# A one-layer gated mixer on one core: mask and one-hot products grouped, one output tile summed in another order, one tile group given more banks

## The chip, the core and the metric

The kernel runs on one core of one Trainium2 chip. A core has TensorE (PE, matrix products into eight PSUM banks), VectorE (DVE), ScalarE (ACT), GpSimd (POOL) and SyncE (SP, which here only issues DMAs). Each engine works through its own instructions in order and waits on semaphores for the others. The metric is the device time of one execution in microseconds (us); the figure to compare is the median of several runs.

## The reference

One decoder layer over 512 tokens of width 1024, all in float32:

```python
def mixer(x, ...):
    proj = x @ w_in                       # q, k, v of three branches and three gate vectors
    o_da  = diff_attention(...)           # 4 heads, two softmax maps each, relative bias
    o_sb  = stick_breaking_attention(...) # 8 heads of 64, strictly causal
    o_dl  = dilated_attention(...)        # 12 heads of 128, windows with stride 1, 4, 16, relative bias
    merged = g0 * (o_da @ w_branch_da) + g1 * (o_sb @ w_branch_sb) + g2 * (o_dl @ w_branch_dil)
    return merged @ w_out

x   = layer_norm(ALPHA * x + mixer(x))
c   = square(relu(x @ w_up)) @ w_down
ple = sigmoid(x @ w_ple_gate) * (p @ w_ple)
x   = layer_norm(ALPHA * x + c + ple)
```

In stick-breaking attention a query sees only earlier keys: `before = k_pos < q_pos` masks the logits. The relative bias is `bias_table[rel_bucket(distance)]`, with 32 buckets and 16 heads that use a bias.

## The kernel before

Nearly every product is split: an operand is held as a high and a low part (each of a type that PE takes at full rate), and three products hi·hi, hi·lo, lo·hi are added in PSUM. A weight chunk of 128×1024 comes by a DMA of SP into a ring tile `raw`, ACT rounds it to `wh` (L243), DVE subtracts to get `wl` (L245), and PE multiplies. Several large products are formed by seven products of sums instead of eight; the sums of weights are added up in DRAM by DMAs of POOL.

The work is one list of `items`. The loop over it emits, for each item, some weight splits (`pump`, whose second argument is how many at most), one step of each attention head in flight (`step`), and the item's products; the result of an item is read out while the next one runs. What stands in an engine's queue in the end is this emission, put in order again by the tile framework, which also chooses the PSUM banks: six banks are for `at_bank()` tiles and two for `mm_bank()` tiles.

The places that the change touches:

- `sb_head` (L1601 on): one head of the stick-breaking branch, eight in all, between 20 and 230 us. It takes three banks for the logits: `bank[2]` holds two key blocks (`kb` 3 and 2) side by side, `bank[1]` and `bank[0]` one each. Per key block it makes a pair of products (`mm_pair`, lines L146 and L147) and then adds the mask by a product of the bf16 identity `identb` with `mask_b` (256 columns for key block 3, 128 for the others; lines L1613 and L1616). ACT (L1628) reads the bank next.
- `rel_vec` and `tables` (L1480, L1519): the bias as a function of distance. The bias table `rel`, split into three bf16 parts on 96 partitions and a row of −1e30 on the 97th, is multiplied with one-hot columns `oh`: five products of four heads each, every one with a bank, an ACT copy (L1485) and a POOL DMA to the DRAM tile `rv` of its own. `shifted` later reads `rv` back.
- `wout_items` (L877): the output projection, per half of the columns four token tiles `tt` of eight contraction steps `k`. Step `k` reads `merged_T[k // 4, tt // 2, ...]`, which `turn_item` makes by four transposes on PE (L794), a cast on ACT (`mh`, L798) and a subtraction on DVE (`ml`, L799). The order of items is tile 0, turns (1,1,·), tile 1, turns (0,1,·), tile 2, tile 3.
- `ple_items` (L945): the embedding product `p @ w_ple`, eight tiles `(half, tt)`, each in an `at_bank()`, read out by ACT (L961). Between them PE transposes the normed tokens (L924), also into `at_bank()` tiles.

Of the kernel before, what the change touches and what calls it, by code (L numbers as in the profile page):

```python
# [12 lines left out]
BF16 = mybir.dt.bfloat16  # L13
# [3 lines left out]
S = 512  # L17
D = 1024
P = 128
# [36 lines left out]
def trunk(tc, a, out):  # L56
    nc = tc.nc
    es = ExitStack()
    with es:
# [14 lines left out]
        def slot(name, dt=F32):  # L74
            return big.tile([P, 512], dt, name=nm(name), tag="s", bufs=NSLOT)
# [7 lines left out]
        def at_bank():  # L83
            return psum.tile([P, 512], F32, name=nm("at"), tag="at", bufs=6)
# [58 lines left out]
        def mm_pair(ps, st, tw, side, cs, cm, start, stop):  # L143

            hi, lo = tw[side]
            nc.tensor.matmul(ps, st[side][:, cs], hi[:, cm], start=start, stop=False, skip_group_check=True)  # L146
            nc.tensor.matmul(ps, st[side][:, cs], lo[:, cm], start=False, stop=stop, skip_group_check=True)  # L147
# [107 lines left out]
        def pump(limit, most=2):  # L255
            n = 0
            while n < most and st["split"] < len(chunks) and st["split"] < limit + RING:
                fill()
                issue_split()
                n += 1  # L260
            fill()
# [4 lines left out]
        def item(cs, mm, ev, need=None, bank=None, size=1.0):  # L266
            items.append({"c": cs, "mm": mm, "ev": ev, "need": need, "bank": bank, "size": size})
# [17 lines left out]
        T = {}  # L285
# [517 lines left out]
        last_plain = len(items)  # L803
# [73 lines left out]
        def wout_items():  # L877
            for half in range(2):
                cs = [chunk(a["wo"][half, c].rearrange("p k n -> p (k n)"), 1024) for c in range(4)]
                for tt in range(4):  # L880
                    def mm(ps, tt=tt, cs=cs):
                        for k in range(8):
                            c = cs[k // 2]
                            s = slice((k % 2) * 512, (k % 2) * 512 + 512)
                            h, lo = merged_T[k // 4, tt // 2, k % 4 // 2]
                            q = slice(k % 2 * 256 + tt % 2 * P, k % 2 * 256 + tt % 2 * P + P)
                            nc.tensor.matmul(ps, h[:, q], c["h"][:, s], start=k == 0, stop=False)
                            nc.tensor.matmul(ps, h[:, q], c["l"][:, s], start=False, stop=False)
                            nc.tensor.matmul(ps, lo[:, q], c["h"][:, s], start=False, stop=k == 7)

                    def ev(ps, tt=tt, half=half):
                        y = xn.pop((tt, half))
                        if not half:
                            x1sum[tt] = small("lsm", 2)
                        i = nc.vector.scalar_tensor_tensor(y, y, ALPHA, ps, op0=OP.mult, op1=OP.add,
                                                           accum_out=x1sum[tt][:, half:half + 1])
                        st["added"] = getattr(i, "ins", i)
                        x1[tt, half] = y
                        if half:
                            pending.append(ln1_gen(tt))  # L900
                    item(cs if tt == 3 else [], mm, ev, need=cs, bank=at_bank)
                    for t in {0: [(1, 1, 0), (1, 1, 1)], 1: [(0, 1, 0), (0, 1, 1)]}.get(tt, ()) if not half else ():
                        turn_item(*t)
# [41 lines left out]
        def ple_items():  # L945
            cs = [chunk(a["wp"][half].rearrange("p k n -> p (k n)"), 1024) for half in range(2)]
            for half in range(2):
                for tt in range(4):
                    def mm(ps, tt=tt, half=half):
                        c = cs[half]  # L950
                        for k in range(2):
                            s = slice(k * 512, k * 512 + 512)
                            q = slice(tt * P, tt * P + P)
                            h, lo = pTs[k]
                            nc.tensor.matmul(ps, h[:, q], c["h"][:, s], start=k == 0, stop=False)
                            nc.tensor.matmul(ps, h[:, q], c["l"][:, s], start=False, stop=False)
                            nc.tensor.matmul(ps, lo[:, q], c["h"][:, s], start=False, stop=k == 1)

                    def ev(ps, tt=tt, half=half):
                        t = slot("ple")  # L960
                        nc.scalar.copy(t, ps)  # L961
                        ple[tt, half] = t
                    item([cs[half]] if tt == 3 else [], mm, ev, need=cs, bank=at_bank)


        sums_first = set()
# [463 lines left out]
        ple_at = len(items)  # L1430
# [17 lines left out]
        identb = one.tile([P, P], BF16, name="identb")  # L1448
# [13 lines left out]
        mask_b = one.tile([P, 2, P], BF16, name="mask_b")  # L1462
# [13 lines left out]
        rel = one.tile([97, 16], BF16, name="rel")  # L1476
        nc.vector.memset(rel[96:97, :], NEG)
        rv = dram.tile([16, 640], F32, name="rv")

        def rel_vec(cols, segs):  # L1480
            for src, d0, n in segs:
                ps = at_bank()
                nc.tensor.matmul(ps[0:4, :n], rel[:, cols], src, start=True, stop=True)
                sb = slot("rvs")[0:4, :]
                nc.scalar.copy(sb[:, :n], ps[0:4, :n])  # L1485
                nc.gpsimd.dma_start(rv[cols, d0:d0 + n], sb[:, :n])
                yield

        def shifted(h0, n, m):
            ts = []  # L1490
# [19 lines left out]
        tab_da = tab_g0 = tab_g1 = tab_g2 = None  # L1510

        oh = []

        def load_onehot():
            oh.extend(slot("oh", BF16) for _ in range(3))
# [2 lines left out]

        def tables():  # L1519
            nonlocal tab_g0, tab_g1, tab_g2  # L1520
            yield from rel_vec(slice(0, 4), [(oh[0][:97, :], 0, 512), (oh[1][:97, 0:128], 512, 128)])
            yield from rel_vec(slice(4, 8), [(oh[1][:97, 128:512], 0, 384)])
            yield from rel_vec(slice(8, 12), [(oh[2][:97, 0:256], 0, 256)])
            yield from rel_vec(slice(12, 16), [(oh[2][:97, 256:512], 0, 256)])
            tab_g0 = shifted(4, 4, 256)
            tab_g1 = shifted(8, 4, 128)
            tab_g2 = shifted(12, 4, 128)
# [34 lines left out]
        def make_lam():  # L1562
            lamt, t, r = lams

            nc.vector.tensor_copy(rel[0:32, :], t)
            nc.vector.tensor_sub(t, t, rel[0:32, :])
            nc.vector.tensor_copy(rel[32:64, :], t)
            nc.vector.tensor_copy(r, rel[32:64, :])
            nc.vector.tensor_sub(t, t, r)
            nc.vector.tensor_copy(rel[64:96, :], t)  # L1570
            lp = one.tile([P, 2], F32, name="lp")
            for i in range(2):
                nc.vector.scalar_tensor_tensor(lamt[:, 2 * i, :], lamt[:, 2 * i, :], 1.0, lamt[:, 2 * i + 1, :],
                                               op0=OP.mult, op1=OP.mult, accum_out=lp[:, i:i + 1])
            nc.scalar.activation(lp, lp, AF.Exp)
            nc.vector.tensor_sub(lam, lp[:, 0:1], lp[:, 1:2])
            nc.vector.tensor_scalar(lam, lam, LAM_INIT, -1.0, op0=OP.add, op1=OP.mult)
            nc.vector.tensor_scalar(gcol, gcol, 1.0 - LAM_INIT, None, op0=OP.mult)
# [22 lines left out]
        def sb_head(hd):  # L1601
            pr, side = hd // 2, hd % 2
# [3 lines left out]
            blk = [(0, 0, 0, 512), (1, 1, 0, 384), (2, 2, 0, 256), (3, 2, 256, 256)]  # L1606
            bank = [at_bank() for _ in range(3)]
            for kb, bi, c0, n in reversed(blk):
                ps = bank[bi][:, c0:c0 + n]
                mm_pair(ps, T["sb_k", pr], T["sb_q", pr], side, slice(kb * P, kb * P + P), slice(S - n, S),  # L1610
                        kb != 2, False)
                if kb == 3:
                    nc.tensor.matmul(ps, identb, mask_b.rearrange("p a b -> p (a b)"), start=False, stop=False,  # L1613
                                     skip_group_check=True)
                else:
                    nc.tensor.matmul(ps[:, 0:P], identb, mask_b[:, 1, :], start=False, stop=False,  # L1616
                                     skip_group_check=True)
            w = [512, 384, 512]
            sph, spl, later = {}, {}, {}
            for bi in (2, 1, 0):  # L1620
                n = w[bi]
                ps = bank[bi][:, :n]
# [9 lines left out]
                h = slot("sph", F32R)[:, :n]  # L1632
                lo = slot("spl", F32R)[:, :n]
# [24 lines left out]
            for kb, bi, c0, n in reversed(blk):  # L1658
                ps = bank[bi][:, c0:c0 + n]
# [305 lines left out]
        for n, it in enumerate(items):  # L1965
# [22 lines left out]
                for _ in range(lead):  # L1988
                    left_step(*preps.popleft())

            pump(freed, {1: 3, 3: 0, 4: 0, ple_at: 0, ple_at + 1: 0}.get(n, 1 if n < 10 else 2))
            if n == 8:
                tie.clear()
            if n == 4:
# [158 lines left out]
```

## Time and profile before

| | |
|---|---|
| median of three runs | 1042.58 us (1042.33 to 1043.28) |
| time of the profiled execution | 1043.19 us |
| its span, first to last instruction | 1041.0 us |
| mean granted clock of TensorE | 0.998 |
| PE busy | 1031.1 us, 99% |
| DVE busy | 787.0 us, 76% |
| ACT busy | 593.2 us, 57% |
| POOL busy | 180.0 us, 17% |

A row of the timeline gives the start, the duration, the engine, the line and operation, the tiles written and read, their shape (for a product first the weights, partitions*columns, then what streams through, partitions x columns) and, in brackets, the idle time ahead with the engine that ended it. Products are pipelined: what one of them costs is read from the start of one row to the start of the next, since the durations overlap. PEld rows are the loads of weights.

### The profile page before, as it was taken

What the parts mean: (1) busy time and instruction counts of PE and PEld (TensorE: products, weight loads), DVE (VectorE), ACT (ScalarE), POOL (GpSimd) and SP (SyncE); (2) the same over time, 40 slices, a digit from 0 to 9 for tenths busy, and PEclk for the clock granted to TensorE, in tenths of its full rate; (3) what the DMA queues carried; (4) which work ended last, traced back from release to release, by engine and by line L of the source; (5) the groups of instructions that cost most, each with busy time, mean ns of one, the idle gap of its engine ahead of it and who ended that gap; (6) DMA issues with size and microseconds to landing.
All of it is one profiled execution on the core that took longest, in us unless ns stands there. A gap on an engine that the chain in (4) does not pass through costs nothing.

```text
span 1041.0 us, 15056 instructions
## 1 busy us (share of the span) xinstructions
PE 1031.1 (99%) x5450; PEld 880.1 (85%) x5450; DVE 787.0 (76%) x1408; ACT 593.2 (57%) x1014; POOL 180.0 (17%) x271
## 2 busy tenths in 40 slices
PE   9999999999999999999999999999999999999997
PEld 6888788889888888888888888889999889889886
DVE  6888577769774667779788895798768877877966
ACT  7566445536344545676575743775666556555651
POOL 0003412031211232411011040111111111111001
PEclk9999999999999999999999999999999999999999
DMA  8449978495985999967889795479999999999612
GB/s 308 121 154 271 255 214 197 128 283 142 278 207 206 258 281 294 248 199 202 251 238 230 269 320 197 147 219 331 320 288 316 296 316 314 306 344 286 201 59 81
DMA packets 71323, 249.21 MB, mean 239 GB/s; under 512 B 8809, under 2 KB 9593, under 8 KB 71249
## 3 DMA queue, kind: packets, MB, share of 16 engines
q0 software_dynamic: 32464, 116.21, 44.7%
q1 hardware_dynamic: 38208, 131.13, 35.2%
q8 instruction: 43, 0.70, 0.3%
q10 hardware_dynamic: 576, 0.92, 0.2%
q14 instruction: 32, 0.25, 0.1%
HBM read 246.10 MB, written 98.59 MB: 331 GB/s over the span
## 4 chain that ended last, share of the span: by engine, by line
PE 94%; DVE 2%; ACT 2%; issue 1%; DMA 0%; POOL 0%; DVEq 0%; POOLq 0%
PE mm L87 10%; PE mm L88 10%; PE mm L89 10%; PE at L1261 4%; PE at L1262 4%; PE at L1263 4%; PE at L599 3%; PE at L601 3%; PE at L600 3%; PE mm L496 2%; PE mm L498 2%; PE mm L497 2%; PE at L89 1%; PE at L87 1%; PE at L88 1%; PE at L761 1%
## 5 line engine op out<-in xcount | busy, mean ns | idle before, releaser
L243 ACT CAST wh<-raw 128x1024 fp32r<-128x1024 f32 x257 | 268.7, 1049 | 241.1 <-PE mm L88 133.6
L245 DVE TENSOR_TENSOR wl<-raw,wh 128x1024 fp32r<-128x1024 f32 x257 | 312.5, 1222 | 112.2 <-ACT wh L243 110.9
L87 PE MATMUL mm<-xhT,wh 128*128 128x512 f32 x302 | 120.0, 397 | 0.0
L89 PE MATMUL mm<-xhT,wl 128*128 128x512 f32 x302 | 118.3, 392 | 0.0
L88 PE MATMUL mm<-xlT,wh 128*128 128x512 f32 x302 | 118.2, 391 | 0.0
L87 PE MATMUL mm<-x1hT,wh 128*128 128x256 f32 x256 | 73.8, 288 | 0.0
L1261 PE MATMUL at<-wh,hh 128*128 128x512 f32 x188 | 73.7, 392 | 0.0
L1262 PE MATMUL at<-wl,hh 128*128 128x512 f32 x188 | 73.7, 392 | 0.0
L1263 PE MATMUL at<-wh,hl 128*128 128x512 f32 x188 | 73.1, 389 | 0.0
L88 PE MATMUL mm<-x1lT,wh 128*128 128x256 f32 x256 | 72.2, 283 | 0.0
L89 PE MATMUL mm<-x1hT,wl 128*128 128x256 f32 x256 | 71.8, 283 | 0.0
L89 PEld LDWEIGHTS mm<-xhT,wl 128*128 128x128 f32 x302 | 56.8, 188 | 12.0
L87 PEld LDWEIGHTS mm<-xhT,wh 128*128 128x128 f32 x302 | 56.8, 188 | 11.3 <-issue 0.4
L88 PEld LDWEIGHTS mm<-xlT,wh 128*128 128x128 f32 x302 | 56.8, 188 | 10.5
L87 PEld LDWEIGHTS mm<-x1hT,wh 128*128 128x128 f32 x256 | 48.8, 190 | 4.8 <-ACT up L1195 2.9
L88 PEld LDWEIGHTS mm<-x1lT,wh 128*128 128x128 f32 x256 | 48.9, 191 | 1.5
L89 PEld LDWEIGHTS mm<-x1hT,wl 128*128 128x128 f32 x256 | 48.6, 191 | 0.0
L1095 POOL DMA_DIRECT2D usum<-in_wu_dram x32 | 28.5, 928 | 103.1 <-DVE wl L245 38.7
L1095 POOL DMA_DIRECT2D dsum<-in_wd_dram x28 | 25.5, 933 | 100.2 <-DVE wl L245 33.3
L1263 PEld LDWEIGHTS at<-wh,hl 128*128 128x128 f32 x188 | 35.3, 188 | 7.6
L1261 PEld LDWEIGHTS at<-wh,hh 128*128 128x128 f32 x188 | 35.5, 189 | 6.0
L1262 PEld LDWEIGHTS at<-wl,hh 128*128 128x128 f32 x188 | 35.5, 189 | 5.6
(601 smaller groups left out, 2686.4 us busy)
## 6 DMA issues: line engine op xcount, KB each, us to landing
usum<-in_wu_dram POOLq DMA_DIRECT2D x48, 512.0 KB, 9.2
dsum<-in_wd_dram POOLq DMA_DIRECT2D x42, 512.0 KB, 9.1
raw<-in_wt_dram SPq DMA_DIRECT2D x38, 512.0 KB, 5.7
raw<-usum SPq DMA_DIRECT2D x32, 512.0 KB, 7.8
raw<-dsum SPq DMA_DIRECT2D x28, 512.0 KB, 8.1
raw<-in_wd_dram SPq DMA_DIRECT2D x25, 512.0 KB, 6.5
raw<-in_wu_dram SPq DMA_DIRECT2D x24, 512.0 KB, 7.2
raw<-in_wv_dram SPq DMA_DIRECT2D x18, 512.0 KB, 5.5
```

Of the source, the lines that this page charges most:

```text
L87: nc.tensor.matmul(ps, wh, xh, start=start, stop=False, skip_group_check=True)
L88: nc.tensor.matmul(ps, wh, xl, start=False, stop=False, skip_group_check=True)
L89: nc.tensor.matmul(ps, wl, xh, start=False, stop=stop, skip_group_check=True)
L243: i = nc.scalar.copy(h, raw)
L245: i = nc.vector.tensor_sub(lo, raw, h.bitcast(F32))
L599: nc.tensor.matmul(ps, h[:, q], c["h"][:, n], start=go, stop=False, skip_group_check=True)
L600: nc.tensor.matmul(ps, h[:, q], c["l"][:, n], start=False, stop=False, skip_group_check=True)
L601: nc.tensor.matmul(ps, lo[:, q], c["h"][:, n], start=False, stop=end, skip_group_check=True)
L1095: i = nc.gpsimd.dma_start(o, i, accum_op=OP.add, max_dma_last_dim=4096)
L1261: nc.tensor.matmul(ps, h[:, q], c["h"][:, s], start=go, stop=False, skip_group_check=True)
L1262: nc.tensor.matmul(ps, h[:, q], c["l"][:, s], start=False, stop=False, skip_group_check=True)
L1263: nc.tensor.matmul(ps, lo[:, q], c["h"][:, s], start=False, stop=end, skip_group_check=True)
```

## The change

Five edits:

1. `sb_head`: the four mask products of a head are issued first, one behind the other, and open the banks; the pairs of products add to them.
2. `rel_vec`: the table is copied three times into `relp` (97 partitions, three groups of 96 columns, zero but for 16 columns at 0, 32 and 64), and three products of 96×512 into one bank take the place of five; one ACT copy of 96 partitions follows, and five DMAs cut the pieces from it. `tables` yields as often as before.
3. `wout_items`: the third tile of the first half sums its steps in the order 4 to 7, then 0 to 3.
4. `ple_items`: tiles with even `tt` go to the two `mm_bank()` banks, the others stay.
5. The main loop: at the item before the first branch `pump` may emit one split instead of two.

```diff
-                        for k in range(8):
+                    ks = (4, 5, 6, 7, 0, 1, 2, 3) if tt == 2 and not half else range(8)
+                        for k in ks:
...
-                    item([cs[half]] if tt == 3 else [], mm, ev, need=cs, bank=at_bank)
+                    item([cs[half]] if tt == 3 else [], mm, ev, need=cs, bank=at_bank if tt % 2 else None)
...
-        def rel_vec(cols, segs):
-            for src, d0, n in segs:
-                ps = at_bank()
-                nc.tensor.matmul(ps[0:4, :n], rel[:, cols], src, start=True, stop=True)
-                sb = slot("rvs")[0:4, :]
-                nc.scalar.copy(sb[:, :n], ps[0:4, :n])
-                nc.gpsimd.dma_start(rv[cols, d0:d0 + n], sb[:, :n])
-                yield
+        def rel_vec():
+            ps = at_bank()[0:96, :]
+            for i in range(3):
+                nc.tensor.matmul(ps, relp[0][:, i, :], oh[i][:97, :], start=i == 0, stop=i == 2)
+            sb = slot("rvs")[0:96, :]
+            nc.scalar.copy(sb, ps)
+            for i, g, c0, d0, n in ((0, 0, 0, 0, 512), (1, 0, 0, 512, 128), (1, 1, 128, 0, 384),
+                                    (2, 2, 0, 0, 256), (2, 3, 256, 0, 256)):
+                r = 32 * i + 4 * g
+                nc.gpsimd.dma_start(rv[4 * g:4 * g + 4, d0:d0 + n], sb[r:r + 4, c0:c0 + n])
...
+            relp.append(slot("relp", BF16)[:97, :288].rearrange("p (i c) -> p i c", i=3))
+            nc.vector.memset(relp[0], 0.0)
+            for i in range(3):
+                nc.vector.tensor_copy(relp[0][:, i, 32 * i:32 * i + 16], rel)
...
             for kb, bi, c0, n in reversed(blk):
-                ps = bank[bi][:, c0:c0 + n]
-                mm_pair(ps, T["sb_k", pr], T["sb_q", pr], side, slice(kb * P, kb * P + P), slice(S - n, S),
-                        kb != 2, False)
-                if kb == 3:
-                    nc.tensor.matmul(ps, identb, mask_b.rearrange("p a b -> p (a b)"), start=False, stop=False,
-                                     skip_group_check=True)
-                else:
-                    nc.tensor.matmul(ps[:, 0:P], identb, mask_b[:, 1, :], start=False, stop=False,
-                                     skip_group_check=True)
+                m = mask_b.rearrange("p a b -> p (a b)") if kb == 3 else mask_b[:, 1, :]
+                nc.tensor.matmul(bank[bi][:, c0:c0 + (n if kb == 3 else P)], identb, m, start=kb != 2, stop=False,
+                                 skip_group_check=True)
+            for kb, bi, c0, n in reversed(blk):
+                mm_pair(bank[bi][:, c0:c0 + n], T["sb_k", pr], T["sb_q", pr], side, slice(kb * P, kb * P + P),
+                        slice(S - n, S), False, False)
...
-            pump(freed, {1: 3, 3: 0, 4: 0, ple_at: 0, ple_at + 1: 0}.get(n, 1 if n < 10 else 2))
+            pump(freed, {1: 3, 3: 0, 4: 0, last_plain - 1: 1, ple_at: 0, ple_at + 1: 0}.get(n, 1 if n < 10 else 2))
```

What the edits move in the queues. First PE at the second stick-breaking head, where its logits begin (`at_600`, `at_599` and `at_598` are its three banks, L496 is the value projection that follows). Before:

```order
L146 MATMUL at_600<-sb_q_359,sb_k_361 128x256
L147 MATMUL at_600<-sb_ql_360,sb_k_361 128x256
L1613 LDWEIGHTS identb
L1613 MATMUL at_600<-mask_b,identb 128x256
L146 MATMUL at_600<-sb_q_359,sb_k_361 128x256
L147 MATMUL at_600<-sb_ql_360,sb_k_361 128x256
L496 MATMUL mm_501<-wh_374,xhT 128x512
```

After, in the same place:

```order
L1620 LDWEIGHTS identb
L1620 MATMUL at_600<-mask_b,identb 128x256
L1620 LDWEIGHTS identb
L1620 MATMUL at_600<-mask_b,identb 128x128
L1620 LDWEIGHTS identb
L1620 MATMUL at_599<-mask_b,identb 128x128
L1620 LDWEIGHTS identb
L1620 MATMUL at_598<-mask_b,identb 128x128
L146 MATMUL at_600<-sb_q_359,sb_k_361 128x256
L147 MATMUL at_600<-sb_ql_360,sb_k_361 128x256
L496 MATMUL mm_501<-wh_374,xhT 128x512
```

All four masks, and loads of the same identity for each, now stand together ahead of the pairs, and the first of them open their banks; here the pair of key block 2 has moved behind the L496 products, together with the pairs of `at_599` and `at_598`, which stood there before. At the other heads the same four rows move ahead of the pairs; at the first and the fourth of them some products of a projection that stand beside them change places too.

Then PE at the third tile of the output projection (`at_1346` before, `at_1339` after), behind the transposes into `mm_1343` (before) and `mm_1336` (after). `mh_1341` and `mh_1334` are casts of the transposes that stand just ahead; `mh_1326` is one of the turns (1,1,·), which follow tile 0. Before:

```order
L794 MATMUL mm_1343_6149<-ident_251,b1_947_4379 128x128
L794 MATMUL mm_1343_6149<-ident_251,b1_955_4409 128x128
L887 MATMUL at_1346_6159<-wh_1280_5869,mh_1341_6145 128x512
L888 MATMUL at_1346_6159<-wl_1281_5870,mh_1341_6145 128x512
```

After:

```order
L794 MATMUL mm_1336_6140<-ident_251,b1_940_4370 128x128
L794 MATMUL mm_1336_6140<-ident_251,b1_948_4400 128x128
L889 MATMUL at_1339_6150<-wh_1287_5920,mh_1326_6090 128x512
L890 MATMUL at_1339_6150<-wl_1288_5921,mh_1326_6090 128x512
L891 MATMUL at_1339_6150<-wh_1287_5920,ml_1327_6091 128x512
```

The first product behind the transposes no longer reads the cast of those transposes; the rows with `mh_1334` now come twelve products later. Edit 5 moves no row on any engine.

More of the change, by code (lines that the diff above doesn't have):

```diff
@@ L880, in wout_items, with mm @@
                 for tt in range(4):
-                    def mm(ps, tt=tt, cs=cs):
-                        for k in range(8):
+                    ks = (4, 5, 6, 7, 0, 1, 2, 3) if tt == 2 and not half else range(8)
+                    def mm(ps, tt=tt, cs=cs, ks=ks):
+                        for k in ks:
                             c = cs[k // 2]
@@ L886, in mm @@
                             q = slice(k % 2 * 256 + tt % 2 * P, k % 2 * 256 + tt % 2 * P + P)
-                            nc.tensor.matmul(ps, h[:, q], c["h"][:, s], start=k == 0, stop=False)
+                            nc.tensor.matmul(ps, h[:, q], c["h"][:, s], start=k == ks[0], stop=False)
                             nc.tensor.matmul(ps, h[:, q], c["l"][:, s], start=False, stop=False)
-                            nc.tensor.matmul(ps, lo[:, q], c["h"][:, s], start=False, stop=k == 7)
+                            nc.tensor.matmul(ps, lo[:, q], c["h"][:, s], start=False, stop=k == ks[-1])
                     def ev(ps, tt=tt, half=half):
@@ L1512, in trunk @@
         oh = []
+        relp = []
         def load_onehot():
@@ L1520, in tables @@
             nonlocal tab_g0, tab_g1, tab_g2
[L1521 to L1524, printed above, removed]
+            yield
+            yield
+            rel_vec()
+            for _ in range(3):
+                yield
             tab_g0 = shifted(4, 4, 256)
```

## The prediction

> **What bounds the kernel.** I read the page's table of engines, then the waits of PE, then PE's timeline where the change works.
>
> ```profile
> PE 1031.1 (99%) x5450; PEld 880.1 (85%) x5450; DVE 787.0 (76%) x1408; ACT 593.2 (57%) x1014; POOL 180.0 (17%) x271
> PE 94%; DVE 2%; ACT 2%; issue 1%; DMA 0%; POOL 0%; DVEq 0%; POOLq 0%
> 0.00:230.00 230.00, 228.43 (x1074) 184.72 (x1075) 168.62 (x297) 126.03 (x202) 42.72 (x72) 1.00 0.74 215
> PE at L1440 <- DVE zero L1437: 1.2, 1, 1.2
> PE mm L690 <- DVE da_klb L101: 0.3, 1, 0.3
> PE at L887 <- ACT mh L798: 0.2, 1, 0.2
> PE mm L496 <- DVE sb_qlb L101: 0.2, 1, 0.2
> PE at L955 <- ACT ple L961: 0.2, 1, 0.2
> ```
>
> PE is busy 99% and carries 94% of the chain that ended last; in the first 230 us, where two of the edits lie, it is busy 228.43 us and DVE 168.62. Its listed waits are five, 2.1 us together. So what PE no longer has to do is taken off the end, unless one of those few waits swallows it; work for DVE, ACT and POOL costs nothing as long as PE does not come to wait for it. The listed idle time understates a wait, since the ends of products are modelled; I measure from start to start. All three wins must come from small steps on PE: about 0.2% (2.1 us) is what a measurement of this kernel can tell from no change.
>
> **Part 1, masks.** One head, the sixth (left out are the second pair of 256 columns, its mask, and the first product of 384):
>
> ```profile
> 144.30 0.28 PE L146 MATMUL at<-sb_qb,sb_kb 128*128 128x256 f32 x1
> 144.41 0.28 PE L147 MATMUL at<-sb_qlb,sb_kb 128*128 128x256 f32 x1
> 144.54 0.28 PE L1613 MATMUL at<-mask_b,identb 128*128 128x256 bf16 x1
> ...
> 145.20 0.34 PE L147 MATMUL at<-sb_qlb,sb_kb 128*128 128x384 f32 x1
> 145.38 0.23 PE L1616 MATMUL at<-mask_b,identb 128*128 128x128 bf16 x1
> 145.42 0.47 PE L146 MATMUL at<-sb_qb,sb_kb 128*128 128x512 f32 x1
> 145.73 0.39 PE L147 MATMUL at<-sb_qlb,sb_kb 128*128 128x512 f32 x1
> 145.96 0.23 PE L1616 MATMUL at<-mask_b,identb 128*128 128x128 bf16 x1
> 146.00 0.47 PE L496 MATMUL mm<-wh,xhT 128*128 128x512 f32 x1
> 146.31 0.39 PE L497 MATMUL mm<-wl,xhT 128*128 128x512 f32 x1
> L1616 PEld LDWEIGHTS <-identb x24: 95/95/98, 21.7 to 194.7; 128*128 128x128 bf16 x24
> ```
>
> Start to start, a product of 256 columns takes 0.12 (144.30 to 144.54, two), of 384 0.18 (145.20), of 512 0.23 (145.73). From 144.30 to 146.31 are 2.01 us; the products in it are 4×0.12 + 2×0.18 + 3×0.225 = 1.515 (0.225 for 512, between the 0.22 and 0.23 that such rows show). The four masks therefore take 0.50: 0.12 for the wide one and 0.13 for each narrow one (145.73 to 146.31, less two of 0.225). But 128 columns should stream in 0.12 − 128×(0.225 − 0.12)/256 = 0.067. The other 0.06 stands behind the mask, where the next product's f32 weights come late: the short mask does not cover their load. In a row, three masks are followed by another identity, whose load is short (95 ns; a load of f32 weights is one of 0.19 us, as in the L87 row further below), and only the last by f32 weights. I estimate 0.12 + 2×0.067 + 0.13 = 0.38, so 0.12 saved per head. Bounds: nothing saved (0.13 each stays) to 0.24 (all 640 columns at the streaming slope, 0.26).
>
> The third to eighth head save 6×0.12 = 0.72. The first two are special:
>
> ```profile
> 30.98 0.28 PE L147 MATMUL at<-sb_ql,sb_k 128*128 128x256 f32 x1
> 31.49 0.47 PE L496 MATMUL mm<-wh,xhT 128*128 128x512 f32 x1 [0.23 <-DVE sb_qlb L101]
> 30.65 0.70 DVE sb_qlb L101
> ```
>
> L496 waits for DVE, which ends at 31.35; 0.51 lies between its row and that ahead, 0.39 too much. What the first head saves ahead of it is waited away. The second head puts three masks more ahead of L496 and one pair behind: behind it, three masks of 0.13 leave and a pair of 0.24 comes, so 0.15 is saved. Part 1: 0.72 + 0.15 = **0.87**, bounds 0.15 to 1.6.
>
> **Part 2, one-hot products.** The first of the five, with its neighbours, and products with 64 columns of weights:
>
> ```profile
> 99.06 0.34 PE L1665 MATMUL at<-sml,ones_r 128*128 128x384 f32 x1
> 99.33 0.38 PE L1483 MATMUL at<-oh,rel 97*4 97x512 bf16 x1
> 99.64 0.50 PE L87 MATMUL mm<-xhT,wh 128*128 128x512 f32 x1
> 99.97 0.39 PE L88 MATMUL mm<-xlT,wh 128*128 128x512 f32 x1
> 99.64 0.19 PEld L87 LDWEIGHTS mm<-xhT,wh 128*128 128x128 f32 x1 [0.23 <-issue]
> L1483 PE MATMUL at<-oh,rel x5: 218/271/377, 99.3 to 113.4; 97*4 97x256 bf16 x2, 97*4 97x512 bf16 x1, 97*4 97x128 bf16 x1, 97*4 97x384 bf16 x1
> 105.86 0.40 PE L1686 MATMUL at<-al,sb_v 128*64 128x512 f32 x1
> 106.10 0.33 PE L1684 MATMUL at<-ah,sb_v 128*128 128x384 f32 x1
> ```
>
> From 99.06 to 99.97 are 0.91; less 0.18 and 0.225 for the neighbours, 0.505 remains, 0.28 above a stream of 512. The load of L87's weights starts only at 99.64, behind the product and not beside it: this product stands alone on PE, with a gap on either side. Five of them carry 1536 columns, as do three of 512, so the streams cancel (0.68 each way) and the gaps decide: five of 0.28 before. After, I count one for the group, so 4×0.28 = **1.12** is saved. Bounds: no gap at all saves 1.40, one for each of the three 0.56. What makes the gap is open: the narrow weights, the 97 rows, or a bank opened behind a separate load. Weights of 64 columns show none (0.24 from 105.86 to the next row), those of 128 neither, which speaks for the 4 columns; 97 rows stay, so I keep one.
>
> The Trainium skill, TensorEngine Tiling, Key Properties, says that a change of tiling mode drains the engine. By that 4 columns (a mode of 32) drain it and 96 (the full array) would not, and the part would save 1.40. The rows with 64 columns of weights, another mode on that page, don't bear the rule out: they change mode at every row without a gap.
>
> The new table `relp` adds a memset and three copies to DVE, in a stretch where DVE idles 61 of 230 us: I count nothing. Each is smaller than the 64x512 row of 0.70 above, so they are under 2.8 us together were that cover gone. ACT has four copies less. POOL's queue issues the same five DMAs, now together behind the third product, and the sums of weights queued behind the first come that much later; POOL is busy 42.72 of these 230 us, and none of PE's listed waits is for it.
>
> **Part 3, third output tile.** Eight transposes ahead of it, and eight elsewhere:
>
> ```profile
> 626.12 1.03 PE L794 MATMUL mm<-ident,b 128*128 128x128 f32 x8
> 627.39 0.50 PE L887 MATMUL at<-wh,mh 128*128 128x512 f32 x1 [0.24 <-ACT mh L798]
> 662.48 1.03 PE L924 MATMUL at<-ident,xn 128*128 128x128 f32 x8
> 663.27 0.48 PE L955 MATMUL at<-wh,pTh 128*128 128x512 f32 x1
> 627.37 1.29 DVE L799 TENSOR_TENSOR ml<-mm,mh 128x512 fp32r<-128x512 f32 x2 [0.36 <-ACT mh L798]
> ```
>
> 1.27 against 0.79: a wait of **0.48** for the cast. After, the tile begins with parts made earlier and needs the new ones twelve products (2.7 us) later, at about 629.6; DVE ends the last at 628.66. The wait goes; bounds 0.4 to 0.5.
>
> **Part 4, embedding tiles.**
>
> ```profile
> 667.22 0.39 PE L957 MATMUL at<-wh,pTl 128*128 128x512 f32 x1
> 667.80 0.50 PE L955 MATMUL at<-wh,pTh 128*128 128x512 f32 x1 [0.20 <-ACT ple L961]
> 668.14 0.39 PE L956 MATMUL at<-wl,pTh 128*128 128x512 f32 x1
> 667.19 0.56 ACT L961 COPY ple<-at 128x512 f32<-128x512 f32 x1
> ```
>
> The fifth tile waits for the ACT copy of the first, whose bank it takes: 0.58 and 0.34 where 0.225 each is due, 0.47 lost. After, tiles 1, 3, 5, 7 share two banks, so the fifth again takes the bank of the first, and ACT copies it at the same place. I forecast **0**; bounds −0.47 (the wait goes) to +0.47 (a second like it). Edit 5 moves no instruction: 0.
>
> **Sum.** 0.87 + 1.12 + 0.48 = 2.47. The profiled execution took 1043.19, 0.61 above the median, and would take 1040.7; from the median, 1042.58 − 2.47 = **1040.1 us**.
>
> **Rivals.**
> 1. *More*: no gap in the one-hot group and no wait in the embedding: 2.47 + 0.28 + 0.47 = 3.2, 1039.4. For it, the rows of 64 columns; against, the shared bank. 0.13.
> 2. *Masks in a row cost as much as apart*: part 1 falls to 0.15, total 1.75, 1040.8. The trace has no two masks in a row, so nothing contradicts it but the short load. 0.12.
> 3. *The 97 rows make the gap*: three gaps, total 1.91, 1040.7. 0.08; with rival 2, 1.19 and 1041.4, 0.03.
> 4. *Slower: a bank opened by a product with a separate load costs a gap.* In this trace only the five one-hot products are that; masks before add to a bank that an f32 pair has opened (144.30, no gap). After, three masks per head open a bank: 24×0.28 = 6.7 lost, net +4.25, 1046.8. It decides from 0.10 per opening mask (2.47/24). Against it: in the 99.33 rows the load behind is late too, which an opening would not cause. 0.10.
>
> The forecast takes 0.54. Some 0.07 of that falls short of 2.1 us by its terms' lower ends, so faster is 0.47 + 0.13 = 0.60, within 0.2% is 0.07 + 0.12 + 0.08 + 0.03 = 0.30, and slower is 0.10. The range 1039.0 to 1041.7 takes in the forecast and rivals 1 to 3, with 0.3 to 0.4 on either side for the scatter of a median (the three runs lie 0.95 apart); beyond it lies rival 4.
>
> **What would show it.** Right: the mask rows 0.07 apart and 0.13 behind the last; L1485 with at most one gap; 0.8 between the transposes near 624 and the next product; L957 still waiting for ACT. Wrong: gaps of 0.2 or more around each mask, a new releaser in PE's waits, or a time above 1042.6.

## The result: 1039.90 us, and where 3.1 us went

| | before | after |
|---|---|---|
| median | 1043.04 us (8 runs, 1042.33 to 1043.54) | 1039.90 us (8 runs, 1039.57 to 1040.78) |
| profiled execution | 1043.19 us, span 1041.0 | 1040.78 us, span 1038.8 |

The ratio is 0.9971, 95% interval 0.9961 to 0.9981. The eight runs of before include the three that were known, and their median lies 0.46 higher. The change is worth 3.14 us from median to median, and 2.41 between the two profiled executions; the end of this section shows why these differ.

The table of engines on the page of after, then PE's waits (total, times, longest):

```profile
PE 1027.6 (99%) x5448; PEld 880.9 (85%) x5448; DVE 787.1 (76%) x1412; ACT 591.7 (57%) x1010; POOL 179.7 (17%) x271
```

```profile
PE at L1442 <- DVE zero L1439: 1.2, 1, 1.2
PE at L761 <- DVE b L772: 1.1, 1, 1.1
PE mm L690 <- DVE da_klb L101: 0.5, 1, 0.5
PE mm L496 <- DVE sb_qlb L101: 0.4, 1, 0.4
PE mm L957 <- ACT ple L963: 0.2, 1, 0.2
```

PE is busy 3.5 us less, DVE the same. The wait of L887 for the cast `mh` has left the list; the waits of L496 and L690 have each grown by 0.2; the one at L761 is new. Now the four places of the change, on PE's timeline of after: a head's row of masks, the one-hot group, the eight transposes ahead of the third w_out tile, and the fifth embedding tile.

```profile
141.54 0.45 PE L1620 MATMUL at<-mask_b,identb 128*128 128x256 bf16 x4
141.80 0.36 PE L146 MATMUL at<-sb_qb,sb_kb 128*128 128x256 f32 x1
142.00 0.28 PE L147 MATMUL at<-sb_qlb,sb_kb 128*128 128x256 f32 x1
142.12 0.28 PE L146 MATMUL at<-sb_qb,sb_kb 128*128 128x256 f32 x1
...
104.94 0.28 PE L1693 MATMUL at<-al,sb_v 128*64 128x256 f32 x1
105.05 0.81 PE L1485 MATMUL at<-oh,relp 97*96 97x512 bf16 x3
105.51 0.59 PE L87 MATMUL mm<-xhT,wh 128*128 128x512 f32 x1
105.94 0.40 PE L88 MATMUL mm<-xlT,wh 128*128 128x512 f32 x1
...
624.42 1.03 PE L794 MATMUL mm<-ident,b 128*128 128x128 f32 x8
625.22 0.48 PE L889 MATMUL at<-wh,mh 128*128 128x512 f32 x1
...
664.99 0.39 PE L959 MATMUL at<-wh,pTl 128*128 128x512 f32 x1
665.59 0.50 PE L957 MATMUL mm<-wh,pTh 128*128 128x512 f32 x1 [0.21 <-ACT ple L963]
665.92 0.39 PE L958 MATMUL mm<-wl,pTh 128*128 128x512 f32 x1
```

- **Masks.** From 141.54 to 142.12 are 0.58; less a pair of 256 columns (2×0.12), the four masks take 0.34. Before they took 0.50. Of the 0.34, 0.26 lies between the first mask and the first pair, and 0.08 behind it (141.80 to 142.00, where 0.12 is due). So 0.16 is saved per head.
- **One-hot.** From 104.94 to 105.94 is 1.00; less 0.12 and 0.225 for the neighbours, the three products take 0.655, and 1536 columns at 0.225 for 512 are 0.675. There is no gap at all. The five of before, read in the same way, took 0.51, 0.36, 0.45, 0.41 and 0.41, together 2.14; about 1.48 is saved by these steps.
- **Third w_out tile.** 624.42 to 625.22 is 0.80, where 1.27 stood: 0.47 saved.
- **Fifth embedding tile.** 0.60 and 0.33 for two products of 0.225: 0.48 lost, as before (0.47), and again behind ACT's copy of the first tile.

The new wait takes back part of this in the profiled execution. PE's timeline of after, then ACT's and DVE's:

```profile
554.83 0.39 PE L600 MATMUL at<-wl,xhT 128*128 128x512 f32 x1
556.35 0.50 PE L761 MATMUL at<-wh,oTh 128*128 128x512 f32 x1 [1.12 <-DVE b L772]
552.78 1.05 ACT L243 CAST wh<-raw 128x1024 fp32r<-128x1024 f32 x1 [5.16 <-DMA raw<-in_wgm_dram]
553.87 1.23 DVE L245 TENSOR_TENSOR wl<-raw,wh 128x1024 fp32r<-128x1024 f32 x1 [1.43 <-ACT wh L243]
555.61 0.68 DVE L772 TENSOR_TENSOR b<-b,at 128x512 f32<-128x512 f32 x1
```

The chain runs through the last three rows: a load of gate weights, which POOL adds to what already lies in its buffer, lands late; ACT, idle for 5.16, casts it; DVE, idle for 1.43 behind that, splits it and only then, in L772, frees the bank that L761 needs. PE loses 1.3 there (554.83 to 556.35, less 0.225). Before's profile, for its part, lost 0.5 in its first 8 us, ahead of every edit: the same product of L347 starts at 7.07 in before and at 6.55 in after. 3.14 + 0.5 − 1.3 is 2.3, near the 2.41. Whether the wait belongs to the kernel is settled by the run `after_again` below.

### The profile page after: what moved, and what is told of

It is laid out like the page before. It is cut to its first block, busy times and chain, and to the rows that moved or that the text cites. A ratio compares the mean times of both kernels' runs of the same rounds, so it can differ in the third digit from the quotient of the medians.

```text
span 1038.8 us, 15050 instructions
## 1 busy us (share of the span) xinstructions
PE 1027.6 (99%) x5448; PEld 880.9 (85%) x5448; DVE 787.1 (76%) x1412; ACT 591.7 (57%) x1010; POOL 179.7 (17%) x271
## 4 chain that ended last, share of the span: by engine, by line
PE 86%; issue 4%; DMA 3%; DVE 3%; ACT 2%; POOL 1%; DVEq 0%; POOLq 0%; ACTq 0%
PE mm L87 10%; PE mm L88 10%; PE mm L89 10%; PE at L1263 4%; PE at L1264 4%; PE at L1265 4%; DMA raw<-in_wgm_dram 2%; PE mm L496 2%; PE mm L498 2%; PE mm L497 2%; PE at L89 1%; PE at L87 1%; PE at L88 1%; PE at L601 1%; PE at L599 1%
## 5 line engine op out<-in xcount | busy, mean ns | idle before, releaser
L87 PE MATMUL mm<-xhT,wh 128*128 128x512 f32 x302 | 119.0, 394 | 0.0
L89 PE MATMUL mm<-xhT,wl 128*128 128x512 f32 x302 | 118.2, 391 | 0.0
L88 PE MATMUL mm<-xlT,wh 128*128 128x512 f32 x302 | 118.2, 391 | 0.0
L87 PE MATMUL mm<-x1hT,wh 128*128 128x256 f32 x256 | 73.7, 288 | 0.0
L88 PE MATMUL mm<-x1lT,wh 128*128 128x256 f32 x256 | 72.2, 283 | 0.0
L89 PE MATMUL mm<-x1hT,wl 128*128 128x256 f32 x256 | 71.8, 283 | 0.0
L89 PEld LDWEIGHTS mm<-xhT,wl 128*128 128x128 f32 x302 | 56.7, 188 | 11.9
L87 PEld LDWEIGHTS mm<-xhT,wh 128*128 128x128 f32 x302 | 56.7, 188 | 11.0
L88 PEld LDWEIGHTS mm<-xlT,wh 128*128 128x128 f32 x302 | 56.8, 188 | 10.8
L87 PEld LDWEIGHTS mm<-x1hT,wh 128*128 128x128 f32 x256 | 48.7, 190 | 4.8 <-ACT up L1197 3.0
L88 PEld LDWEIGHTS mm<-x1lT,wh 128*128 128x128 f32 x256 | 48.8, 191 | 1.5
L89 PEld LDWEIGHTS mm<-x1hT,wl 128*128 128x128 f32 x256 | 48.6, 191 | 0.0
```

Of the source, the lines that this page charges most:

```text
L87: nc.tensor.matmul(ps, wh, xh, start=start, stop=False, skip_group_check=True)
L88: nc.tensor.matmul(ps, wh, xl, start=False, stop=False, skip_group_check=True)
L89: nc.tensor.matmul(ps, wl, xh, start=False, stop=stop, skip_group_check=True)
```

## The experiments

**Each edit alone.** My theory was that PE sets the time, so that the steps taken off PE come off the end, less what the few waits swallow. Four kernels, all on one chip with 33 runs of before (median 1042.99), each being before with one edit of the diff:

```
masks_alone   the loop over blk in sb_head split in two: first four masks, then four pairs
onehot_alone  relp, rel_vec() and tables() as after
wout_alone    ks = (4, 5, 6, 7, 0, 1, 2, 3) for tt == 2 of the first half
emb_alone     bank=at_bank if tt % 2 else None
```

> The kernel before with the masks edit alone. My theory (PE sets the time; what counts is PE's steps from start to start): the four masks take 0.34 per head in a row and 0.50 apart, so 8 heads lose 1.36 of steps, of which some 0.2 goes into a longer wait of L496 for sb_ql at the first head: 1.1 to 1.2 faster. The prediction's own size for this edit was 0.87. Rival: masks in a row cost as much as apart, and the gain of the whole change comes from elsewhere: 0 to 0.15 faster. Rival: an opening mask costs a gap: slower.

> The kernel before with the one-hot edit alone. My theory: five gaps of 0.28 go and no new one comes, so the group of three takes 0.65 to 0.70 on PE: 1.4 to 1.5 faster. The prediction's size was 1.12 (one gap stays). Rival: the products are covered by waits behind them, so that the time moves by under 0.5.

> The kernel before with the other order of halves in the third w_out tile alone. My theory: the wait for the cast behind eight transposes goes, 1.27 from start to start becomes 0.8: 0.4 to 0.5 faster. Rival: the tile then waits for ml, the low part that DVE ends last, twelve products later: 0.

> The kernel before with the embedding tiles over both bank pools alone. My theory: the fifth tile takes the first tile's bank again, now one of two, and waits for the same ACT copy: 0.0, within 0.15, with L955 still waiting for ple. Rival: the wait at the fifth tile goes or halves: 0.2 to 0.47 faster. Rival: a second tile waits as well: up to 0.47 slower.

| kernel | median (11 runs) | against before | ratio, 95% interval |
|---|---|---|---|
| masks_alone | 1042.18 | −0.81 | 0.9990 (0.9981 to 0.9999) |
| onehot_alone | 1041.28 | −1.71 | 0.9982 (0.9973 to 0.9991) |
| wout_alone | 1042.61 | −0.38 | 0.9994 (0.9985 to 1.0003) |
| emb_alone | 1043.19 | +0.20 | 0.9998 (0.9990 to 1.0007) |

The sum is −2.70, where the whole change gave −3.14; with intervals of ±0.9 on each, that is no contradiction. Only masks and one-hot are faster beyond their intervals.

The traces tell the edits apart more sharply than the medians. The same product is looked up in two profiles; the difference of its starts is PE's lead over before at that place, and what an edit is worth is the growth of the lead across it:

| start in before | masks_alone | onehot_alone | wout_alone | emb_alone | after_again |
|---|---|---|---|---|---|
| 20.05 (L88) | 0.59 | 0.59 | 0.57 | 0.72 | 0.56 |
| 84.18 (L89) | 0.80 | 0.54 | 0.57 | 0.70 | 0.80 |
| 242.55 (L465) | 1.56 | 2.22 | 0.56 | 0.70 | 3.23 |
| 600.00 (L761) | 1.57 | 2.15 | 0.57 | 0.69 | 3.22 |
| 690.15 (L1017) | 1.56 | 2.12 | 1.05 | 0.68 | 3.72 |

The lead in the first row is before's slow start and no edit's work. From there the masks are worth 0.97, the one-hot edit 1.68 (2.22 less 0.54, of which 0.1 is lost again later), the third w_out tile 0.48 and the embedding tiles nothing: 3.1 together, and 3.16 in `after_again`, which is the kernel after. So the edits add up to the whole change.

For w_out the step itself is 1.27 before and 0.79 now (625.58 to 626.37). In emb_alone the fifth tile still waits for ACT, for 0.2 by the list of waits. The masks gave less than 8×0.16 = 1.3: the first two heads gave 0.10 (the lead is 0.69 at 40.07), the other six 0.87. The one-hot edit gave 0.2 more than the five steps above show. A part of this stands in the products behind each narrow one, which were taken at 0.225 and are a little slower: two steps behind the last one in before are 0.24 (113.94, 114.18, 114.42).

**Why the one-hot gap went.** Before's five lone products with other widths of weights (zero columns added), then with other rows, and after's three products with narrow weights:

```
onehot_widths      relw = zeros, 4 used columns; widths = [4, 32, 64, 96, 128], 97 rows each
onehot_rows        columns x rows = (128, 97), (64, 128), (64, 97), (4, 128), (96, 128)
onehot_narrow_row  matmul(banks[i], rel, oh[i][:97, :], start=True, stop=True), 16 columns, a bank each
```

> The kernel before; the five one-hot products, each alone between f32 products as before, have weights of 4, 32, 64, 96 and 128 columns in this order (the added columns are zeros, and only the first four rows of the result are used). Streams of 512, 128, 384, 256, 256 columns. Theory of narrow weights: the gap of 0.28 stands at 4 and 32 columns and is gone from 64 on. Theory of 97 rows: 0.28 at all five. Theory of the lone product (a bank opened with a separate short load between f32 products): 0.28 at all five.

> The kernel before, five lone one-hot products with weights of 128 columns x 97 rows, 64 x 128, 64 x 97, 4 x 128 and 96 x 128 (padded with zeros). If the gap hangs on 64 columns or fewer whatever the rows: none, 0.28, 0.28, 0.28, none. If 97 rows are needed for it: none, none, 0.28, none, none. If it was the place in the program and not the width (the products of 96 and 128 columns stood last before): 0.28 at the first, none at the last two.

> The kernel after, but the three one-hot products in a row have weights of 16 columns and a bank each, in place of 96 padded columns and one bank. Theory that narrow weights drain PE at each change to or from them: one gap for the group, 0.65 + 0.28 = 0.93 from the row ahead to the row behind. Theory that each narrow product costs its own gap: three, 0.65 + 0.84 = 1.5. Theory that what counts is standing alone and not the width: 0.65, as with 96 columns.

PE's timeline of onehot_widths: the products with 64 and with 96 columns of weights, with their neighbours.

```profile
106.79 0.28 PE L1694 MATMUL at<-al,sb_v 128*64 128x256 f32 x1
107.00 0.35 PE L1485 MATMUL at<-oh,relw 97*64 97x384 bf16 x1
107.28 0.50 PE L87 MATMUL mm<-xhT,wh 128*128 128x512 f32 x1
107.62 0.40 PE L88 MATMUL mm<-xlT,wh 128*128 128x512 f32 x1
...
110.63 0.39 PE L89 MATMUL mm<-xhT,wl 128*128 128x512 f32 x1
110.85 0.27 PE L1485 MATMUL at<-oh,relw 97*96 97x256 bf16 x1
110.88 0.47 PE L87 MATMUL mm<-xhT,wh 128*128 128x512 f32 x1
111.19 0.39 PE L88 MATMUL mm<-xlT,wh 128*128 128x512 f32 x1
```

With 64 columns: 0.83 less 0.12 and 0.225 leaves 0.485 for 384 columns that stream in 0.17, a gap of 0.31. With 96: 0.56 less 0.45 leaves 0.11 for 256 columns, none. All five read in this way, stream taken off at 0.225 for 512 columns:

| weights, columns x rows | 4x97 | 32x97 | 64x97 | 96x97 | 128x97 | 64x128 | 4x128 | 96x128 |
|---|---|---|---|---|---|---|---|---|
| gap, us | 0.28 | 0.30 | 0.31 | none | none | 0.32 | 0.29 | none |

(The 128x97 product stood last in one kernel and first in the other: none both times.) So neither the 97 rows nor the lone bank makes the gap, nor the place in the program: 64 columns or fewer do. My theory had the border between 32 and 64, and missed. (The time of onehot_rows, 1043.13, holds a wait of 1.2 at L87 for DVE, near 94 us, which before doesn't have; that run gives DVE more to clear. The steps read here don't contain it.)

The Trainium skill, TensorEngine Tiling, Key Properties, says that a change of tiling mode drains the engine. The bf16 rows agree: weights that need at most 64 of the columns cost 0.28 to 0.32 at a visit, 96 and 128 nothing. The f32 rows of 64 columns (`al`, quoted in the prediction) show no gap. No row says in which mode a product ran, so the drain itself isn't shown, nor what sets the f32 rows apart.

onehot_narrow_row, the same view:

```profile
105.49 0.28 PE L1690 MATMUL at<-al,sb_v 128*64 128x256 f32 x1
105.70 0.60 PE L1485 MATMUL at<-oh,rel 97*16 97x512 bf16 x2
106.23 0.50 PE L87 MATMUL mm<-xhT,wh 128*128 128x512 f32 x1
106.57 0.40 PE L88 MATMUL mm<-xlT,wh 128*128 128x512 f32 x1
...
109.18 0.38 PE L1485 MATMUL at<-oh,rel 97*16 97x512 bf16 x1
```

Two narrow products in a row take 1.08 − 0.12 − 0.225 = 0.735 for a stream of 0.45: one gap of 0.28 for both. The third came 3.5 us later, alone (the three did not stay together, so the group's 0.93 that I expected has no row), and cost 0.28 again (108.86 to 109.82 between the rows of L89 and L88, less 0.45 and 0.225). The gap is paid per visit, not per product. Padding to 96 columns removed it; putting the products together would have left one.

**Why the mask row is cheap.** After with three forms in three pairs of heads:

```
heads 3, 4:  for x in reversed(blk): mask(*x, x[0] != 2); pair(*x, False)
heads 5, 6:  for x in reversed(blk): pair(*x, x[0] != 2)
             for x in reversed(blk): mask(*x, False)
the others:  as after
```

> The kernel after with three forms of the masks: heads 1, 2, 7, 8 as after (row of four ahead of the pairs, opening the banks); heads 3, 4 each mask ahead of its own pair (opening, but apart); heads 5, 6 a row of four behind the pairs (adding, but in a row). My theory (the load of the f32 weights behind a lone short mask is what costs): 0.34 per head as after, 0.50 apart though opening, 0.34 in a row though adding. Rival (opening the bank with the mask is what makes it cheap): 0.34, 0.34, 0.50.

PE's timeline of mask_forms, head 3 (first and last mask) and head 5:

```profile
69.84 0.28 PE L1622 MATMUL at<-mask_b,identb 128*128 128x256 bf16 x1
69.88 0.36 PE L146 MATMUL at<-sb_qa,sb_ka 128*128 128x256 f32 x1
...
71.03 0.23 PE L1622 MATMUL at<-mask_b,identb 128*128 128x128 bf16 x1
71.07 0.48 PE L146 MATMUL at<-sb_qa,sb_ka 128*128 128x512 f32 x1
71.39 0.40 PE L147 MATMUL at<-sb_qla,sb_ka 128*128 128x512 f32 x1
71.62 0.39 PE L87 MATMUL mm<-xhT,wh 128*128 128x512 f32 x1
...
118.96 0.45 PE L1622 MATMUL at<-mask_b,identb 128*128 128x256 bf16 x4
119.22 0.48 PE L87 MATMUL mm<-xhT,wh 128*128 128x512 f32 x1
119.53 0.39 PE L88 MATMUL mm<-xlT,wh 128*128 128x512 f32 x1
```

Opening but apart: from 69.84 to 71.62 are 1.78, less pairs of 4×0.12 + 2×0.18 + 2×0.225 = 1.29: 0.49. In a row but adding: 0.57 − 0.225 = 0.345. Head 7, as after, has 0.34. So the row saves, and opening the banks neither costs nor saves; the slower rival of the prediction has no price. PE's lead over before says the same of the heads not quoted: it grows by 0.57 across heads 5 to 8 (2.28 at 120.05, 2.85 at 195.03), 0.14 each.

Each lone narrow mask takes 0.13, and what it costs beyond its stream shows at the next f32 product (71.07 to 71.39 is 0.32, where 0.23 is due). That it is the load of the f32 weights which the short mask doesn't cover fits the rows but is argued. A fixed price of the change from a bf16 to an f32 product is not it: behind the mask of 256 columns there is the same change, and that mask takes 0.12, its stream.

**The wait near 555 us, and a version that beats both.** The fifth embedding tile was given a bank freed long before:

```
-bank=at_bank if tt % 2 else None
+bank=at_bank if 4 * half + tt in (1, 3, 4, 7) else None
```

> The kernel after, with the embedding tiles 1, 3, 4, 7 (counted from 0) in the pool of six banks and 0, 2, 5, 6 in that of two, so that the fifth (number 4) takes a bank freed long before and the sixth takes the first's bank 1.4 later. My theory: the wait of 0.37 to 0.47 at the fifth tile goes and no other takes its place: 0.4 faster than after (1039.5 where after has 1039.9). Rival: ACT, which copies the tiles late, makes the sixth or seventh wait instead: 0. At the gate loads near 555 us the theory that the wait there is one of single executions, when the load lands late, expects it in some profiles of kernels with this lead and not in others; the rival expects 1.1 in each.

It ran at 1038.80 (5 runs, 1038.43 to 1038.97), ratio 0.9961 (0.9947 to 0.9975). That is 1.1 under after's 1039.90, but from another set of runs, so both ran once more side by side, with after less its embedding edit (`bank=at_bank` for all tiles):

> The kernel after once more, beside the two below on one chip. If the wait of 1.1 at L761 is one of single executions (the second POOL load of the gate weights lands 7.3 after its issue in that profile, 4.2 to 6.1 in eight others), this profile shows a landing of 4 to 6 and no wait, and the runs lie near 1039.7 with a few 1 above. If it belongs to the kernel, the wait is there again.

> The kernel after with embedding tile 4 in the larger pool and 5 and 6 in the smaller, as in fifth_tile. If its gain is the wait at the fifth tile alone: 0.4 to 0.5 faster than after_again. If fifth_tile's 1038.8 had a second cause: about 1.1 faster.

> The kernel after with the embedding tiles all in the larger pool again, as before. Theory (the embedding edit is worth nothing): as after_again within 0.2. Rival (it pays only together with the third w_out tile, which shifts ACT's work): 0.2 to 0.5 slower than after_again.

| kernel | median | range | ratio, 95% interval |
|---|---|---|---|
| before | 1043.06 (11 runs) | 1042.37 to 1043.66 | |
| after_again | 1039.52 (6) | 1039.34 to 1040.43 | 0.9968 (0.9956 to 0.9979) |
| after_no_emb | 1039.64 (6) | 1039.15 to 1040.04 | 0.9967 (0.9955 to 0.9979) |
| fifth_again | 1039.00 (5) | 1038.86 to 1039.17 | 0.9962 (0.9950 to 0.9975) |

PE's timeline of fifth_again at the fifth tile, and ACT's copy of the first:

```profile
663.88 0.39 PE L959 MATMUL at<-wh,pTl 128*128 128x512 f32 x1
664.11 0.39 PE L957 MATMUL at<-wh,pTh 128*128 128x512 f32 x1
663.86 0.57 ACT L963 COPY ple<-mm 128x512 f32<-128x512 f32 x1
```

0.23 from row to row: the wait is gone, and no tile behind waits. ACT is as late as ever: its copy of the first tile ends at 664.43, after the fifth tile has begun. All five runs lie under all six of after_again (one of after_no_emb is as low, 1039.15); the medians differ by 0.52, the size of the lost 0.48, though the intervals against before overlap. That this version beats after is therefore shown by the step and the order of the runs, not by the intervals. The second cause that 1038.80 suggested did not come back. Undoing the embedding edit moves the median by 0.12, less than the scatter of the runs: it is worth nothing that shows.

The line of POOL's gate loads (L176, 540 to 552 us) gives their time from issue to landing, first in after, then in after_again:

```profile
DMA to landing us min/median/max: 10.8/10.9/11.1
```

```profile
DMA to landing us min/median/max: 7.9/8.0/8.1
```

In after_again there is no wait at L761. In the other twelve profiles the median is 7.3 to 9.7, and none of them waits there (before has 9.2, onehot_narrow_row 9.7). The load that ACT waits for is the first of the two, issued at 541.93 in after and landed 10.8 later, at its cast of 552.78; the expectation above counted from the issue of the second.

PE's lead is not what brings the wait out, since POOL issues the load as much earlier as PE is ahead. POOL's issue in after, then in before, and in before the row of DVE that frees the bank and the product that takes it:

```profile
541.93 0.87 POOL L176 DMA_DIRECT2D raw<-in_wgm_dram  x1 [1.90 <-DVE wl L245]
545.08 0.87 POOL L176 DMA_DIRECT2D raw<-in_wgm_dram  x1 [1.91 <-DVE wl L245]
557.25 0.68 DVE L772 TENSOR_TENSOR b<-b,at 128x512 f32<-128x512 f32 x1
558.20 0.40 PE L761 MATMUL at<-wh,oTh 128*128 128x512 f32 x1
```

The issue is 3.15 earlier in after, as PE is. In before the bank came free 0.27 ahead of its product (557.93, 558.20) with a landing of 9.2; the 10.9 of after is 1.7 longer. So the wait belongs to executions in which these loads land late. Why they do so was not settled; the other POOL loads of that stretch land late in after too (`usum` 10.7 and `dsum` 14.3, against 8.3 and 11.2 in after_again).

Of the fourteen runs of after in the two sets, ten lie at 1039.34 to 1039.93 and four at 1040.39 to 1040.78, about 1 higher; the profiled one is among the four. Whether the other three waited there has no trace, and it is not the only way to lose time: the profile of after_no_emb, at 1040.04 the slowest of its six runs, has no wait at L761, but one of 0.5 at L146 for ACT, near 21 us.

## Why the prediction was right, and which steps were off

The forecast was 1040.1 with a range of 1039.0 to 1041.7; the median of after is 1039.9. The mechanism held: PE bounds, so steps taken off it come off the end. Its two errors partly cancelled: the sum was too small (2.47 against 3.14), and the median of three that it started from was 0.46 low.

1. **Masks**, 0.87: by the lead it was 0.97. The row of 0.38 measures 0.34, so 0.16 per head and not 0.12 (0.14 to 0.15 by the lead). The mis-sized step is the streaming time of a 128-column mask: 0.067, drawn from f32 rows, holds a fixed part per product that the row of four doesn't show (0.26 for 640 columns, the sum at the bare slope, which stood as the bound). The gap behind the last mask is there (0.08).
2. **First two heads**: what L496 loses grew as said in after, from 0.39 to 0.58, and to 0.45 in after_again; in masks_alone it did not grow (0.36). Of the 0.32 that the two heads' rows save, 0.10 remained in masks_alone and after_again and 0.13 in after (the lead from 20.05 to 40.07); 0.15 was the forecast.
3. **One-hot**, 1.12: the step that failed is "97 rows stay, so I keep one". The rows have no part in it. The group has no gap and saves 1.48 by its steps and 1.68 by the lead: this is the term that the forecast had most wrong. The rule of the Trainium skill, 1.40, came nearer than my choice, and rival 1 was right in this half. The work that `relp` adds to DVE was rightly counted as nothing: it takes 0.50 there (0.18 and 0.32 from 82.50 on), and no wait of PE comes of it.
4. **Third w_out tile**, 0.48: 0.47 by the step; DVE's low part came in time.
5. **Embedding**, 0: right, with the waiting tile and its releaser named.
6. **Rivals.** Rival 2 (masks in a row cost as much) and rival 4 (an opening mask costs a gap) fall with 0.34 per head; rival 3 falls with the table of widths.
7. **A new releaser in PE's waits** stood under "wrong", and one came: L761 behind DVE. The prediction read only what PE waited for, not how near the loads of the branch weights came to being waited for: before's profile has ACT idle 3.51 for the same load, and PE 0.27 short of a wait. What made the difference is a landing of 10.9 instead of 9.2 in that execution, and no run ties it to the edits.

## What to carry to other kernels

Where one engine is busy 99%, read it from start to start: lone short products cost more than they stream, and the same products in a row, or padded until they use most of the array's columns, give that back. Before counting the gain, look up where this engine meets work of another that doesn't move along with it, as L496 met DVE's in the first head; a load whose issue moves along keeps its distance. A wait that moves between two pools of banks is the same wait until the late copy itself is passed by. Judge gains of 0.05% by the step in the trace and by runs side by side on one chip: start-up and landings scatter by as much.

## What the runs showed of the chip

- A lone bf16 product with 4 to 64 columns of weights, between f32 products of 128, costs about 0.3 us beyond its stream, with 97 rows as with 128; with 96 or 128 columns it costs none; two narrow ones of 16 columns in a row pay once.
- Four bf16 masks with the same weights in a row stream without a fixed part per product: 640 columns in 0.26, and 0.08 more behind the last.
- A POOL load of 512 KB at the same place took 7.3 to 10.9 us to land (medians in fourteen profiles), and 10.9 and 8.0 in two executions of the same kernel.
